# The first gather of a mixture-of-experts layer in two halves, with six more dummy products in the sort before it

## The chip, the core and the metric

The kernel runs on one core of a Trainium2 chip. The metric is the device time of one execution in microseconds (us). One core has a matrix engine (PE, with its weight loads listed apart as PEld), a vector engine (DVE), a scalar engine (ACT), a general engine (POOL) and a queue engine (SP) that issues most of the DMA transfers. Each engine works through its own instructions in program order and waits for others through semaphores.

## The reference

One encoder layer for 512 tokens of width 1024: three token mixers (neighbourhood attention, grouped-query attention, attention into memory tokens) that are gated and summed, a layer norm, a mixture of 16 experts, and a second layer norm. What matters here is the mixture. Each expert chooses its 64 tokens:

```python
def expert_choice_ffn(x, w_router, w_gate_up, w_down):
    B, T, D = x.shape
    cap = EC_CAPACITY_FACTOR * T // N_EXPERTS          # 64
    logits = jnp.einsum('btd,de->bte', x, w_router, ...)
    aff = jax.nn.softmax(logits, axis=-1)
    gate, idx = lax.top_k(jnp.swapaxes(aff, 1, 2), cap)
    xs = x[bidx, idx]                                  # the gather
    h = jnp.einsum('becd,edf->becf', xs, w_gate_up)
    hg, hu = jnp.split(h, 2, axis=-1)
    ye = jnp.einsum('becf,efd->becd', jax.nn.silu(hg) * hu, w_down)
    ye = ye * gate[..., None].astype(ye.dtype)
    return jnp.zeros_like(x).at[bidx, idx].add(ye)
```

Everything is float32. The weights of one expert are 8 MB for gate and up and 4 MB for down.

## The kernel before

The first part of the kernel (to about 500 us) computes the token mixers and the router's logits. Then comes the **sort**: the affinities of all tokens are transposed to one row per expert, and DVE takes the 64 largest of each row, eight at a time (`rounds`, lines 1088 to 1097). The smallest of them is the expert's threshold. It is spread to all partitions by a small product on PE (`thp`, line 1170), DVE compares (`msk`, lines 1174 and 1175), PE counts the chosen tokens with triangular matrices (`cnp`, lines 1179 and 1182), and DVE makes from the counts each chosen token's slot number (`pos`, lines 1184 and 1185).

During the sort PE has little of its own to do. `keep_warm(n)` (line 1110) issues n products of the identity with itself, whose result nobody reads; each is two instructions on PE. One such call, `keep_warm(28)` at line 1156, stands on PE's queue right before `thp`. Two smaller ones stand behind `thp` and behind the counts.

The **gather** is done on PE for a quad of four experts at a time, 256 slots. `onehot(qd)` (line 1194) makes on DVE, for each of the four token blocks, a 128x256 matrix in float16 that is 1 where a token sits in a slot. `gather(qd)` (line 1208) is a generator of nine steps: for each of the eight 128-row pieces f of the model width it multiplies the tokens' high halves (`XH`, line 1216) and low halves (`XL`, line 1218), as stationary operands, with the four one-hot blocks, eight products of 256 columns into a PSUM buffer of the tag "mm" (three buffers), and evicts the sum to `xs` on DVE for even f and on ACT for odd f. The ninth step makes the gate values of the slots: small products into a PSUM tile of the tag "Y" (one buffer, line 1232), which DVE reduces (line 1239) into `gw`.

Then follow the **experts**, e = 0 to 15. `gate_up(e, (k,))` (line 1245) multiplies piece k of `xs` with the weights of gate (g) and up (u), k = 0 to 7. `act_h(e)` applies the activation. `h_transpose(e - 1)` transposes the previous expert's hidden values, and `down(e - 1)` (line 1277) multiplies them with the down weights into a PSUM tile of the tag "Y" (line 1287). In the loop, expert 0 has its eight k steps alone; an expert e from 1 to 14 does k = 0 to 3, with `h_transpose(e - 1)` ahead of k = 3, then `down(e - 1)`, for odd e `slots_T` (line 1307, products of 128 columns from one-hot and identity), and then k = 4 to 7.

The first gather runs three of its steps ahead of expert 0 and the others between expert 0's k steps. The gathers of the other three quads are made at the ends of experts 3, 7 and 11.

The **weights** stream through a ring of twelve SBUF buffers of one or two MB (`RING`, line 32; `class Ring`, line 771; its transfers are issued by SP at line 795). The stream is cut into blocks in the order of use; the first twelve are issued as the buffers come free of what the first part of the kernel held in them. Ten of the twelve buffers are used again. Block 12 and those behind it are issued when PE is done with the block whose buffer they take. Since the order of use is gate and up of expert 0 (k = 0 to 7), gate and up of expert 1 (k = 0 to 3), down of expert 0 (0 to 3), and gate and up of expert 1 (k = 4 to 7), blocks 12 to 15 take the buffers of expert 0's k pairs, 16 and 17 those of expert 1's k = 0, 1 and 2, 3, and 18 that of the last piece of expert 0's down weights and expert 1's k = 4. SP issues in order.

PE's order around the change, before: `keep_warm(28)`, `thp`, `keep_warm(1)`, counts, `keep_warm(4)`, gather steps f = 0, 1, 2, then k = 0, f = 3, k = 1, f = 4, and so on to f = 7 behind k = 4, the gate sums behind k = 5, k = 6, k = 7; then expert 1: k = 0, 1, 2, `h_transpose(0)`, k = 3, `down(0)`, `slots_T(0)`, k = 4 to 7.

Of the kernel before, what the change touches and what calls it, by code (L numbers as in the profile page):

```python
# [11 lines left out]
F16 = mybir.dt.float16  # L12
I32 = mybir.dt.int32
AF = mybir.ActivationFunctionType
ALU = mybir.AluOpType
# [3 lines left out]
P = 128  # L19
# [3 lines left out]
NT = 4  # L23
NEXP = 16
CAP = 64
# [11 lines left out]
A_SCALE = 16384.0  # L37
# [22 lines left out]
def layer_kernel(ctx: ExitStack, tc: tile.TileContext, xt, xn, first0, wu, bgate, rpb, gains, wrt,  # L60
                 lnp, lnt, wx, csn, nmask, tri, iota, out, dbg=None):
    nc = tc.nc
# [12 lines left out]
    def R(tag, shape, name, dt=F32, bufs=None):  # L75
        return rp.tile(shape, dt, name=name, tag=tag, bufs=bufs)
# [3 lines left out]
    def PB(tag, name, shape=(P, 512)):  # L80
        return ps.tile(list(shape), F32, name=name, tag=tag, bufs=PS_BUFS[tag])

    def small(shape, name, dt=F32, bufs=2):
        return sp.tile(shape, dt, name=name, tag=name, bufs=bufs)
# [161 lines left out]
    iota_t = cp.tile([P, CAP], F32, name="iota_t")  # L246
# [636 lines left out]
    pos = rt[:, 1].rearrange("p (m e) -> p m e", m=NT)  # L883
# [162 lines left out]
    def x1_parts(m):  # L1046
        nc.scalar.copy(XH[:, m], x1(m))
        for h in range(2):
            c = slice(h * 512, h * 512 + 512)
            nc.gpsimd.tensor_tensor(XL[:, m, c], x1(m)[:, c], XH[:, m, c], op=ALU.subtract)  # L1050

    xhl = R("G0", [P, 2, NT, D], "xhl", F16)
    XH, XL = xhl[:, 0], xhl[:, 1]
# [45 lines left out]
    def steps(*gens):  # L1099
        for g in gens:  # L1100
            next(g, None)

    def all_of(g):
        for _ in g:
            pass
# [4 lines left out]
    def keep_warm(n):  # L1110
        warm2 = PB("T", "warm2")
        for _ in range(n):
            nc.tensor.matmul(warm2[:, :P], ident, ident, start=True, stop=True)
# [39 lines left out]
    for m in (2, 3):  # L1153
        x1_norm(m)
        x1_parts(m)
    keep_warm(28)
    ring.upto(len(RING))
    dump("aff", aff)

# [31 lines left out]

    OH, XS, GW = {}, {}, {}

    def onehot(qd):
        OH[qd] = oh = R("oh", [P, NT, 256], f"oh{qd}", F16)
        for m in range(NT):
            nc.vector.tensor_tensor(oh[:, m].rearrange("p (e s) -> p e s", e=4),
                                    iota_t[:, None, :].to_broadcast([P, 4, CAP]),
                                    pos[:, m, 4 * qd:4 * qd + 4, None].to_broadcast([P, 4, CAP]), op=ALU.is_equal)

    def split_aff():
        a, b = (R("t", [P, NT * NEXP], n, bufs=2).rearrange("p (m e) -> p m e", m=NT) for n in ("affs", "affr"))
        nc.scalar.activation(aff3[:, :, :, 0], aff, AF.Copy, scale=A_SCALE)
        nc.vector.scalar_tensor_tensor(a, aff, A_SCALE, aff3[:, :, :, 0], op0=ALU.mult, op1=ALU.subtract)
        nc.scalar.copy(aff3[:, :, :, 1], a)
        nc.vector.scalar_tensor_tensor(aff3[:, :, :, 2], a, 1.0, aff3[:, :, :, 1], op0=ALU.mult, op1=ALU.subtract)

    def gather(qd):
        oh = OH[qd]
        xs = [R("hi", [P, 4, 256], f"xs{qd}{j}", bufs=2) for j in range(2)]  # L1210
        XS[qd] = xs
        for f in range(KD):
            g = PB("mm", f"ga{qd}{f}")[:, :256]
            c = slice(f * P, (f + 1) * P)
            for m in range(NT):
                nc.tensor.matmul(g, XH[:, m, c], oh[:, m], start=(m == 0), stop=False)  # L1216
            for m in range(NT):
                nc.tensor.matmul(g, XL[:, m, c], oh[:, m], start=False, stop=(m == NT - 1))
            dst = xs[f // 4][:, f % 4]
            if f % 2:  # L1220
                nc.scalar.activation(dst, g, AF.Identity, bias=lnT[:, 1, f:f + 1], scale=gT[:, f:f + 1])
            else:
                nc.vector.tensor_scalar(dst, g, gT[:, f:f + 1], lnT[:, 1, f:f + 1], op0=ALU.mult, op1=ALU.add)
            yield
        if qd == 0:
            split_aff()
        GW[qd] = gw = small([P, 4], "gw", bufs=2)
        gp2 = PB("Y", f"gw{qd}").rearrange("p (i c) -> p i c", i=2)
        for i in range(0, 4, 2):
            gp = gp2[:, i // 2]  # L1230
            for m in range(NT):
                nc.tensor.matmul(gp[:, 0:6], oh[:, m, i * CAP:(i + 2) * CAP],
                                 aff3[:, m, 4 * qd + i:4 * qd + i + 2].rearrange("p e a -> p (e a)"),
                                 start=(m == 0), stop=(m == NT - 1))
        for i in range(0, 4, 2):
            gp = gp2[:, i // 2]
            for j in range(2):
                for b in (0, 64):
                    nc.vector.tensor_reduce(gw[b:b + 64, i + j:i + j + 1], gp[j * 64:j * 64 + 64, 3 * j:3 * j + 3],
                                            axis=AX.X, op=ALU.add)  # L1240
        nc.vector.tensor_scalar(gw, gw, 0.5 / A_SCALE, None, op0=ALU.mult)

    GU, HT, YP = {}, {}, {}

    def gate_up(e, ks):
        qd, i = divmod(e, 4)
        if ks[0] == 0:
            GU[e] = (PB("S", f"g{e}"), PB("T", f"u{e}"))
        for k in ks:
            w = ring.get("gu", e, k)  # L1250
            xs = XS[qd][k // 4][:, k % 4, i * CAP:(i + 1) * CAP]
            for b in range(2):
                for hf in range(2):
                    nc.tensor.matmul(GU[e][b][hf * 64:hf * 64 + 64], xs,  # L1254
                                     w[b][:, hf * 512:hf * 512 + 512],
                                     start=(k == 0), stop=(k == KD - 1))
            ring.done("gu", e, k)
# [89 lines left out]
    def combine(pr):  # L1347
        yh, yl = YP.pop(pr)
        g = GT.pop(pr)
        for m in range(NT):  # L1350
            for o in range(2):
                c = slice(o * 512, (o + 1) * 512)
                cb = PB("mm", f"cb{pr}{m}{o}")
                nc.tensor.matmul(cb, g[:, m], yh[:, c], start=True, stop=False)
                nc.tensor.matmul(cb, g[:, m], yl[:, c], start=False, stop=True)  # L1355
                a = acc_of(m)[:, c]
                nc.vector.tensor_tensor(a, a, cb, op=ALU.add)  # L1357
                yield

    def rows_of_norm(g2):  # L1360
        for h in range(2):
            bc = ln_row(2, h, f"g2{h}")
            yield
            nc.scalar.copy(g2[:, h * 512:(h + 1) * 512], bc)
# [154 lines left out]
            finish(m, 0)  # L1519
            finish(m, 1)  # L1520

    onehot(0)
    g0 = gather(0)
    steps(g0, g0, g0)
    side = iter(())
    for e in range(NEXP):
        if e == 0:
            for k in range(KD):
                gate_up(0, (k,))
                steps(g0)  # L1530
            all_of(g0)
        elif e < NEXP - 1:
            if e == 2:
                side = residual()
            elif e == 3:
                side = combine(0)
            if e == 12:
                g2 = R("G0", [P, D], "ln2g")
                nc.scalar.copy(ident_r, ident)
                side = rows_of_norm(g2)  # L1540
            for k in range(4):
                if k == 3:
                    h_transpose(e - 1)
                gate_up(e, (k,))
                steps(side, side)
            if e % 2 or e == 12:
                all_of(side)
            down(e - 1)
            if e % 2:
                slots_T(e // 2)  # L1550
            if e % 4 == 3:
                onehot(e // 4 + 1)
            for k in range(4, KD):
                gate_up(e, (k,))
                if e == 2:
                    steps(side, side)
                elif e % 2 == 0 and k > 4:
                    if k == 5:
                        side = combine(e // 2 - 1)
                    steps(side, side, side)  # L1560
            all_of(side)
        else:
            sizes = dict(RING)
            pair, one = sorted(ring.free_at_end[:2], key=lambda t: -sizes[t])
            ap12 = R(pair, [P, 2, 2, NT, 256], "accp12", F32R)
            split_acc(1, ap12[:, 0])
            split_acc(2, ap12[:, 1])
            gate_up(e, range(4))
            x0 = [PB(b, f"xq0{mp}", (P, 2, 256)) for mp, b in enumerate("ST")]
            h_transpose(e - 1)  # L1570
            slots_T(e // 2)
            split_acc(3, R(one, [P, 2, NT, 256], "accp3", F32R))
            gate_up(e, (4, 5))
            x1q = preload(1, ("mm", "mm"))
            gate_up(e, (6, 7))
            spare = PB("mm", "spare")
        act_h(e)
        if e % 4 == 3 and e < NEXP - 1:
            all_of(gather(e // 4 + 1))
# [149 lines left out]
```

## Time and profile before

| | |
|---|---|
| median of 3 runs | 977.68 us (976.96 to 979.64) |
| the profiled execution's own time | 977.92 us |
| its span in the profile | 976.1 us |
| PE busy | 944.4 us (97%) |
| DVE busy | 451.9 us (46%) |
| ACT busy | 274.3 us (28%) |
| POOL busy | 78.4 us (8%) |
| bytes moved by DMA | 251.62 MB, mean 258 GB/s |

Busy times count an engine's instructions; a busy PE is not PE at its peak, since products are pipelined. A row of a timeline or of a group of instructions names the start, the duration, the engine, the line, the operation, the tiles (written <- read), their shapes and how many instructions were merged (x4). A row of windows gives for each stretch the busy time and instruction count of PE, PEld, DVE, ACT and POOL, then the granted clock of PE (1.00 is full speed), the DMA engines' busy share and the GB/s that they moved. Everything is told from one profiled execution.

### The profile page before, as it was taken

The page shows a single profiled execution, that of the slowest core. Times are in us where ns is not written, and L with a number is a line of the kernel's source. Part 1 is how long each engine was busy: PE and PEld are TensorE (multiplying, and loading weights), DVE is VectorE, ACT ScalarE, POOL GpSimd, SP SyncE. Part 2 cuts the span into 40 slices and gives each one's busy share as a digit, 9 for nine tenths or more (in the row PEclk, how much of TensorE's full clock was granted, in tenths as well). Part 3 has the DMA queues.
Part 4 walks back from the last instruction along what each step waited for, and adds up shares of the span by engine and source line. Part 5 has one row for each costly group of instructions (what it writes and reads, how often), then busy time and mean ns, then how long its engine had stood idle before and what let it go on. Part 6 is the DMA issues. An engine that isn't in the chain of part 4 may idle for free.

```text
span 976.1 us, 13068 instructions
## 1 busy us (share of the span) xinstructions
PE 944.4 (97%) x5350; PEld 615.0 (63%) x5350; DVE 451.9 (46%) x857; ACT 274.3 (28%) x540; POOL 78.4 (8%) x86
## 2 busy tenths in 40 slices
PE   8999899999999999999999999999999998997996
PEld 8899787889888888887886333433343332432344
DVE  6347678765376566237464155331332222231426
ACT  5343345444354454323223000100010000100123
POOL 0002403000032231000013000000000000000003
PEclk9999999999999999999999999999999999999998
DMA  9312121111333322584719999999999999999992
GB/s 357 111 68 65 65 65 44 65 44 58 85 117 111 101 82 75 217 325 183 279 50 389 389 422 430 430 433 429 429 430 430 430 430 431 432 429 431 428 419 100
DMA packets 38473, 251.62 MB, mean 258 GB/s; under 512 B 12543, under 2 KB 12927, under 8 KB 24590
## 3 DMA queue, kind: packets, MB, share of 16 engines
q1 hardware_dynamic: 37982, 249.74, 63.5%
q10 hardware_dynamic: 432, 1.05, 0.3%
q8 instruction: 42, 0.69, 0.3%
q14 instruction: 17, 0.14, 0.0%
HBM read 247.89 MB, written 2.10 MB: 256 GB/s over the span
## 4 chain that ended last, share of the span: by engine, by line
PE 70%; DMA 18%; DVE 6%; ACT 2%; POOL 2%; issue 1%; SPq 0%; DVEq 0%; POOLq 0%; ACTq 0%
DMA w<-in_wx 17%; PE g L1254 7%; PE u L1254 7%; PE y L1287 6%; PE gate L269 4%; PE gate L271 4%; PE gate L270 4%; PE nqk L271 1%; PE nqk L270 1%; PE nqk L269 1%; PE gy L627 1%; PE pr L269 1%; PE pr L270 1%; PE pr L271 1%; PE ga L1216 1%
## 5 line engine op out<-in xcount | busy, mean ns | idle before, releaser
L1254 PE MATMUL g<-w,xs 128*64 128x512 f32 x512 | 134.7, 604 | 7.5 <-DMA w<-in_wx 7.5
L1254 PE MATMUL u<-w,xs 128*64 128x512 f32 x512 | 131.6, 592 | 0.0
L1287 PE MATMUL y<-w,hT 128*64 128x512 f32 x480 | 107.0, 594 | 4.6 <-DMA w<-in_wx 3.9
L87 ACT CAST y<-y 64x512 fp32r<-64x512 f32 x30 | 17.4, 579 | 240.3 <-PE y L1287 229.0
L88 DVE TENSOR_TENSOR y<-y,y 64x512 fp32r<-64x512 f32 x30 | 20.7, 689 | 135.2 <-ACT y L87 135.2
L1254 PEld LDWEIGHTS u<-w,xs 128*64 128x64 f32 x512 | 36.8, 137 | 73.1 <-issue 71.7
L1287 PEld LDWEIGHTS y<-w,hT 128*64 128x64 f32 x480 | 33.7, 137 | 74.4 <-issue 63.4
L88 DVE TENSOR_TENSOR los<-raw_twin,whi 128x1024 fp32r<-128x1024 f32 x43 | 54.0, 1257 | 51.3 <-ACT whi L87 51.0
L271 PE MATMUL gate<-xh,los 128*128 128x512 f32 x192 | 74.8, 390 | 0.0
L1254 PEld LDWEIGHTS g<-w,xs 128*64 128x64 f32 x512 | 31.3, 136 | 63.7 <-issue 48.0
L269 PE MATMUL gate<-xh,whi 128*128 128x512 f32 x160 | 63.6, 398 | 0.0
L270 PE MATMUL gate<-xl,whi 128*128 128x512 f32 x160 | 62.4, 390 | 0.0
L1357 DVE TENSOR_TENSOR acc<-acc,cb 128x512 f32<-128x512 f32 x56 | 35.4, 683 | 34.5 <-PE cb L1355 34.5
L87 ACT CAST whi<-raw_twin 128x1024 fp32r<-128x1024 f32 x43 | 45.2, 1051 | 7.3 <-PE wo L1062 4.4
L88 DVE TENSOR_TENSOR los<-raw_twin,los 128x1024 fp32r<-128x1024 f32 x21 | 27.4, 1305 | 36.6 <-ACT los L87 36.5
L1426 POOL TENSOR_TENSOR acc<-acc,ln2g 128x512 f32<-128x512 f32 x6 | 7.6, 1279 | 435.4 <-issue 433.4
L271 PEld LDWEIGHTS gate<-xh,los 128*128 128x128 f32 x192 | 36.1, 188 | 7.7
L603 ACT ACTIVATE att_twin<-gs,nm 128x512 f32<-128x512 f32 x32 | 21.7, 683 | 51.4 <-DVE nm L602 51.4
L1264 ACT ACTIVATE tg<-g 128x512 f32<-128x512 f32 x16 | 9.6, 597 | 94.0 <-PE g L1254 94.0
L1275 DVE COPY hT<-ht 128x512 f32<-128x512 f32 x15 | 10.4, 690 | 54.6 <-PE ht L1272 54.6
L269 PEld LDWEIGHTS gate<-xh,whi 128*128 128x128 f32 x160 | 30.0, 188 | 7.5 <-issue 1.0
L270 PEld LDWEIGHTS gate<-xl,whi 128*128 128x128 f32 x160 | 30.1, 188 | 5.9
(405 smaller groups left out, 1883.9 us busy)
## 6 DMA issues: line engine op xcount, KB each, us to landing
w<-in_wx SPq DMA_DIRECT2D x86, 2048.0 KB
raw_twin<-in_wu SPq DMA_DIRECT2D x65, 512.0 KB
w<-in_wx SPq DMA_DIRECT2D x20, 1024.0 KB
raw<-in_wu SPq DMA_DIRECT2D x8, 512.0 KB
xr<-in_xt SPq DMA_DIRECT2D x4, 512.0 KB
macc<-in_xn SPq DMA_DIRECT2D x2, 1024.0 KB
first<-in_first SPq DMA_DIRECT2D x4, 384.0 KB
bf<-in_rpb SPq DMA_DIRECT2D x64, 24.0 KB
```

The costliest lines, as they stand in the source:

```text
L87: nc.scalar.copy(hi, src)
L88: nc.vector.tensor_tensor(lo, src, hi.bitcast(F32), op=ALU.subtract)
L269: nc.tensor.matmul(acc, w_h, rh[:, k], start=(k == 0), stop=False)
L270: nc.tensor.matmul(acc, w_h, rl[:, k], start=False, stop=False)
L271: nc.tensor.matmul(acc, w_l, rh[:, k], start=False, stop=(k == nk - 1))
L603: nc.scalar.activation(self.p[:, h], self.s[h], AF.Exp, bias=nm[:, h:h + 1], accum_out=self.sm[:, h:h + 1])
L627: nc.tensor.matmul(self.y[h * 64:h * 64 + 64, :P], ST["vg"][:, kc, kvh * 64:kvh * 64 + 64], self.pt[:, h, kc], start=(kc == 0), stop=(kc = ...
L1216: nc.tensor.matmul(g, XH[:, m, c], oh[:, m], start=(m == 0), stop=False)
L1254: nc.tensor.matmul(GU[e][b][hf * 64:hf * 64 + 64], xs, w[b][:, hf * 512:hf * 512 + 512], start=(k == 0), stop=(k == KD - 1))
L1275: nc.vector.tensor_copy(t, tp)
L1287: nc.tensor.matmul(y[o * 64:o * 64 + 64], hT[:, c, hf * 64:hf * 64 + 64], w[j][:, o * 512:(o + 1) * 512], start=(k == 0 and j == 0), stop= ...
L1357: nc.vector.tensor_tensor(a, a, cb, op=ALU.add)
```

## The change

The one-hot and the gather take two more arguments, the first expert of the quad and how many experts, so that a part of the quad's slots can be made. The first quad is made in two halves of 128 slots. The first half (experts 0 and 1) is made where the whole was. The second half's one-hot (experts 2 and 3) is issued on DVE behind the first three steps of the first half; its gather is made in expert 1, two steps behind each of k = 0 to 3, and its gate sums behind the last of these, ahead of `down(0)`. The other three quads are made whole, as before. `keep_warm(28)` becomes `keep_warm(34)`.

```diff
-    keep_warm(28)
+    keep_warm(34)
...
-    def onehot(qd):
-        OH[qd] = oh = R("oh", [P, NT, 256], f"oh{qd}", F16)
+    def onehot(qd, e0=0, n=4):
+        if e0 == 0:
+            OH[qd] = R("oh", [P, NT, 256], f"oh{qd}", F16)
+        oh = OH[qd][:, :, e0 * CAP:(e0 + n) * CAP]
         for m in range(NT):
-            nc.vector.tensor_tensor(oh[:, m].rearrange("p (e s) -> p e s", e=4),
-                                    iota_t[:, None, :].to_broadcast([P, 4, CAP]),
-                                    pos[:, m, 4 * qd:4 * qd + 4, None].to_broadcast([P, 4, CAP]), op=ALU.is_equal)
+            nc.vector.tensor_tensor(oh[:, m].rearrange("p (e s) -> p e s", e=n),
+                                    iota_t[:, None, :].to_broadcast([P, n, CAP]),
+                                    pos[:, m, 4 * qd + e0:4 * qd + e0 + n, None].to_broadcast([P, n, CAP]), op=ALU.is_equal)
...
-    def gather(qd):
+    def gather(qd, e0=0, n=4):
         oh = OH[qd]
-        xs = [R("hi", [P, 4, 256], f"xs{qd}{j}", bufs=2) for j in range(2)]
-        XS[qd] = xs
+        if e0 == 0:
+            XS[qd] = [R("hi", [P, 4, 256], f"xs{qd}{j}", bufs=2) for j in range(2)]
+            GW[qd] = small([P, 4], "gw", bufs=2)
+        xs, gw = XS[qd], GW[qd]
+        sl = slice(e0 * CAP, (e0 + n) * CAP)
         for f in range(KD):
-            g = PB("mm", f"ga{qd}{f}")[:, :256]
+            g = PB("mm", f"ga{qd}{f}")[:, :n * CAP]
             c = slice(f * P, (f + 1) * P)
             for m in range(NT):
-                nc.tensor.matmul(g, XH[:, m, c], oh[:, m], start=(m == 0), stop=False)
+                nc.tensor.matmul(g, XH[:, m, c], oh[:, m, sl], start=(m == 0), stop=False)
             for m in range(NT):
-                nc.tensor.matmul(g, XL[:, m, c], oh[:, m], start=False, stop=(m == NT - 1))
-            dst = xs[f // 4][:, f % 4]
+                nc.tensor.matmul(g, XL[:, m, c], oh[:, m, sl], start=False, stop=(m == NT - 1))
+            dst = xs[f // 4][:, f % 4, sl]
...
-        if qd == 0:
+        if qd == 0 and e0 == 0:
             split_aff()
-        GW[qd] = gw = small([P, 4], "gw", bufs=2)
-        gp2 = PB("Y", f"gw{qd}").rearrange("p (i c) -> p i c", i=2)
-        for i in range(0, 4, 2):
+        gp2 = PB("Y", f"gw{qd}{e0}").rearrange("p (i c) -> p i c", i=2)
+        pairs = range(e0, e0 + n, 2)
+        for i in pairs:
...
-        for i in range(0, 4, 2):
+        for i in pairs:
...
-        nc.vector.tensor_scalar(gw, gw, 0.5 / A_SCALE, None, op0=ALU.mult)
+        gs = gw[:, e0:e0 + n]
+        nc.vector.tensor_scalar(gs, gs, 0.5 / A_SCALE, None, op0=ALU.mult)
...
-    onehot(0)
-    g0 = gather(0)
+    onehot(0, 0, 2)
+    g0 = gather(0, 0, 2)
     steps(g0, g0, g0)
+    onehot(0, 2, 2)
+    g1 = gather(0, 2, 2)
     side = iter(())
...
                 gate_up(e, (k,))
                 steps(side, side)
+                if e == 1:
+                    steps(g1, g1)
+            if e == 1:
+                all_of(g1)
             if e % 2 or e == 12:
                 all_of(side)
             down(e - 1)
```

## The prediction

> **What bounds the kernel now.** I read the page first, then wide windows, the weight queue's issues, and the timeline of the stretch that the diff touches.
>
> ```profile
> span 976.1 us, 13068 instructions
> PEclk9999999999999999999999999999999999999998
> GB/s 357 111 68 65 65 65 44 65 44 58 85 117 111 101 82 75 217 325 183 279 50 389 389 422 430 430 433 429 429 430 430 430 430 431 432 429 431 428 419 100
> PE 70%; DMA 18%; DVE 6%; ACT 2%; POOL 2%; issue 1%; SPq 0%; DVEq 0%; POOLq 0%; ACTq 0%
> ```
>
> PE is busy nearly throughout and leads the chain, so at first sight saved PE time is saved time. The GB/s line says otherwise: from its 24th slice on, the weight stream holds about 430. The chain counts a transfer from issue to landing, so it puts time spent behind other transfers elsewhere; for the second half I trust the windows (after the sum of PE and the other engines: granted clock, DMA share, GB/s).
>
> ```profile
> 512.00:529.00 17.00, 15.79 (x141) 13.25 (x140) 9.56 (x37) 7.34 (x12) 8.33 (x10) 0.90 1.01 429
> 529.00:566.50 37.50, 37.50 (x200) 13.90 (x198) 6.51 (x18) 4.53 (x9) 0.00 (x0) 1.00 0.95 374
> 566.00:946.00 380.00, 367.86 (x1786) 140.42 (x1782) 116.62 (x199) 40.94 (x71) 0.00 (x0) 1.00 1.01 430
> ```
>
> From 566 to 946 us the transfers are saturated. What the change does earlier reaches the end only through one number: **when the stream becomes continuous**. From 529 to 566.5 us it runs at 374, a loss of 37.5 x (1 - 374/430) = 4.9 us. That is the most there is to win. Who holds it back there?
>
> ```profile
> 532.40 0.33 SPq L795 DMA_DIRECT2D w<-in_wx  x1
> 538.09 0.33 SPq L795 DMA_DIRECT2D w<-in_wx  x1
> 543.78 0.33 SPq L795 DMA_DIRECT2D w<-in_wx  x1
> 547.65 0.33 SPq L795 DMA_DIRECT2D w<-in_wx  x1
> 551.09 0.33 SPq L795 DMA_DIRECT2D w<-in_wx  x1
> 555.26 0.33 SPq L795 DMA_DIRECT2D w<-in_wx  x1
> 564.32 0.33 SPq L795 DMA_DIRECT2D w<-in_wx  x1
> SPq L795 <- PE u L1254: 41.3, 9, 9.7
> 532.00:533.00 1.00, 1.00 (x9) 0.65 (x8) 0.00 (x0) 0.00 (x0) 0.00 (x0) 1.00 0.16 66
> 533.00:534.00 1.00, 1.00 (x8) 0.40 (x7) 0.54 (x1) 0.00 (x0) 0.00 (x0) 1.00 0.97 213
> 566.00:567.00 1.00, 1.00 (x6) 0.28 (x4) 0.00 (x0) 0.00 (x0) 0.00 (x0) 1.00 0.80 311
> ```
>
> These seven issues are the ring's blocks 12 to 18. Each waits for PE to finish with the block whose place it takes: 12 to 15 after expert 0's k = 1, 3, 5, 7; 16 and 17 after expert 1's k = 1 and 3; 18 after expert 1's k = 4, which stands behind down(0). Block 12 found the stream dry: 66 and 213 GB/s in the two us after its issue, so an issue must come about 2 us before the last landing. Block 18 came with nothing to spare: the rate dips to 311 just two us after its issue. A PE that reaches that point later delays every later byte; one that reaches it earlier helps only as far as those blocks also land.
>
> **The change part by part.** The sum follows PE from the sort to that point.
>
> ```profile
> 513.25 6.41 PE L1113 MATMUL warm<-ident 128*128 128x128 f32 x56
> 520.59 0.39 PE L1170 MATMUL thp<-dg,rt 16*128 16x16 f32 x2 [0.93 <-ACT dg L1168]
> 522.50:526.00 3.50, 3.50 (x19) 2.81 (x19) 2.08 (x7) 0.00 (x0) 0.00 (x0) 0.51 0.99 414
> 522.74 0.22 DVE L1185 TENSOR_TENSOR rt<-rt 128x64 f32<-128x64 f32 x1
> 522.99 1.43 DVE L1197 TENSOR_TENSOR oh<-iota_t,rt 128x256 f16<-128x256 f32 x4
> L1113 PE MATMUL warm<-ident x94: 271/275/423, 507.9 to 523.6; 128*128 128x128 f32 x94
> L1197 DVE TENSOR_TENSOR oh<-iota_t,rt x16: 409/412/424, 523.0 to 824.0; 128x256 f16<-128x256 f32 x16
> ```
>
> Six dummies are 12 instructions of (6.41 - 0.275)/55 = 0.112 us, 1.34 us. The gap they fill is 0.93 us and ends with thp at 520.59; the last dummy now issues at 519.38 + 1.34 = 520.72, thp can follow at 520.83, so thp, the counts and the one-hot come **0.24 us later**. (Bounds: 0, if the gap swallows them, to 0.41 us, 1.34 less 0.93.)
>
> In return the half clock of 522.5 to 526.0 (0.51) should go. It follows the one stretch of the sort in which PE stands still and then runs tiny products. With the gap filled I take full clock; the other case is a rival below. The Trainium skill, in "TensorE: Matmul & The Clock Gate", Part 1 on the clock gate, has the clock fall only after an idle window of about 3.4 us; by that, 0.93 us could not have cost it and filling the gap could not cure it, and the sum would be 0.8 us higher. The trace disagrees: the clock did fall after 0.93 us.
>
> The one-hot of 128 columns is in no row: between 64 columns (0.22) and 256 (0.41), so 0.28 us; four back to back take 1.43 for 256 (0.41 + 3 x 0.34) and 0.28 + 3 x 0.215 = 0.93 for 128, saving 0.50 (bounds 0.3 to 0.75). The first half is ready at 522.99 + 0.24 + 0.93 = 524.16 instead of 524.42. The second half runs on DVE behind the second eviction, under expert 0's first products, and ends near 527, some 3 us before the next gather that DVE has to evict: nothing.
>
> Now the gathers.
>
> ```profile
> 527.57 1.08 PE L1254 MATMUL g<-w,xs 128*64 128x512 f32 x4
> 529.44 0.61 PE L1216 MATMUL ga<-oh,xhl 128*128 128x256 f16 x4
> 530.42 1.08 PE L1254 MATMUL g<-w,xs 128*64 128x512 f32 x4
> 545.73 1.03 PE L1254 MATMUL g<-w,xs 128*64 128x512 f32 x4
> 547.44 1.03 PE L1254 MATMUL g<-w,xs 128*64 128x512 f32 x4
> L1216 PE MATMUL ga<-oh,xhl x128: 272/273/421, 523.8 to 837.2; 128*128 128x256 f16 x128
> 562.02 0.40 PE L1307 MATMUL gT<-id,oh 128*128 128x128 f16 x4
> L1307 PE MATMUL gT<-id,oh x32: 219/219/231, 562.0 to 929.1; 128*128 128x128 f16 x32
> ```
>
> A k step with a gather takes 530.42 - 527.57 = 2.85, without one 547.44 - 545.73 = 1.71: a gather costs 1.14. Its eight products step (0.61 - 0.273)/3 = 0.11 apart, 0.88; the other 0.26 is the change of operands, paid once per insertion. For 128 columns the same kind of product (f16, own weights) stands in L1307: (0.40 - 0.219)/3 = 0.060, in a short run; half of 0.11 is 0.055. I take 0.057: a half gather costs 0.46 + 0.26, that is **0.42 less** than a whole one. The Trainium skill gives about 81 ns for such pairs at 128 columns ("TensorE: Matmul & The Clock Gate", Back-to-back issue gap); L1307's 60 ns speaks against it, and what it would do is the fourth rival.
>
> Before expert 0's first product stand the rest of the first gather and two more: 21 products from the one-hot's end, 527.57 - 524.42 = 3.15 us at half and whole clock. New: 0.04 + 21 x 0.057 + 0.10 = 1.34. The first product comes at 524.16 + 1.34 = 525.50, **2.07 earlier**. The five gathers inside expert 0 give 5 x 0.42 = 2.1; half the gate sums 0.1. Expert 0 ends **4.27 us earlier**.
>
> Then expert 1 pays. Four pairs of half gathers, one insertion each: 4 x (16 x 0.057 + 0.26) = **4.65**. Evictions lie under the products: a pair fills two of three buffers of "mm" and the next pair is 1.7 us of products away; an eviction takes about half a us. The second gate sums cost 0.1 more, and a new wait.
>
> ```profile
> 543.68 0.35 PE L1232 MATMUL gw<-aff,oh 128*128 128x6 f16 x8
> 544.07 1.36 DVE L1239 TENSOR_REDUCE gw<-gw 64x1 f32<-64x3 f32 x8 [0.50 <-PE gw L1232]
> 530.53 0.56 ACT L1221 ACTIVATE xs<-ga,lnT,gT 128x256 f32<-128x256 f32 x1 [3.16 <-PE ga L1218]
> ```
>
> "Y" has one buffer. In expert 0 its four reductions lay under later products; now down(0), the next user of "Y", stands right behind the sums and waits: drain 0.17, start of DVE 0.04, four reductions of 0.17, 0.05 back, less the 0.13 that PE needs anyway, **0.8 us** (bounds 0.5, if the two engines overlap, to 1.2, if an eviction is still ahead on DVE). Queued behind it on PE are down(0), slots_T and expert 1's k = 4, so block 18.
>
> Issues become: 12 at 529.9, 13 at 534.8, 14 at 539.6, 15 at 543.4, 16 at 548.0, 17 at 554.5, and 18 at 564.32 - 4.27 + 4.65 + 0.1 + 0.8 = **565.6**. At 2.1 MB per block and 430 GB/s (4.88 us) blocks 12 to 17 now run gapless from 532.5 to 561.8, and then the stream stands until about 567.6. The old small gaps are traded for one of 6 us, which ends 1.3 us later than the stream became continuous before. Everything behind is transfer-bound, so the end moves by **+1.3 us**: 977.92 (this profiled execution, span 976.1 and 1.8 around it) + 1.3 = **979.2 us**. The median is 977.68, 0.24 below, and its runs span 976.96 to 979.64.
>
> **The rivals.**
>
> 1. Faster. Block 18 is not what sets the end and the 4.7 us by which block 17 lands earlier (561.8 against 566.5) are kept, less little: 977.9 - 4.5 = 973.4. It needs block 18's issue by 559.8. For: every transfer ahead of it does come earlier. Against: the wait on "PE u" is the queue's own account, and PE's work up to that point does not shrink by 5 us.
>
> 2. The dummies don't hold the clock. From 524.2 to 525.93, 16 products step 0.107 instead of 0.057: +0.8, 980.0. For: counts and tiny products stay as they are. Against: the window before 522.5 gains 1.1 us of work.
>
> 3. The halves are tied together. If a product reading one half of an xs tile waits for evictions into the other, expert 1's k = 1 and 2 each wait for drain 0.22, eviction 0.4 and 0.1 of signals: +1.3, 980.5; more where several such waits meet. Against: the product at 530.42 started before ACT's eviction into the same tile (530.53).
>
> 4. Half gathers don't halve. At 0.081 per product the 21 before expert 0, its 40 and expert 1's 64 cost 125 x 0.024 = 3.0 more: 982.2, slower than the bound below. L1307's row is against it, but only four in a row.
>
> **How the numbers follow.** Forecast 0.50, rivals 0.09, 0.19, 0.15, 0.07. A measurement of this kernel tells about 0.3%, 2.9 us, from no change: 974.8 to 980.6. Slower: all of rival 4, two thirds of 3 (with the bounds of the stall), four tenths of 2, and a fifth of the forecast by its bounds and the runs' own spread: 0.07 + 0.10 + 0.07 + 0.10 = 0.34. Faster: rival 1 and 0.01, 0.10. The rest, 0.56, is within. The forecast's own range is 977.8 to 980.8 (stall -0.3 to +0.4, dummies -0.24 to +0.17, one-hot -0.25 to +0.2, 125 products at 0.055 to 0.060 -0.25 to +0.4, so PE's +1.3 becomes +0.2 to +2.5, and some 0.4 of run to run). For 8 in 10 it must take in rivals 2 and 3 and the edge of 4: 976.6 to 981.9.
>
> **What would show it.** Granted clock 1.0 through 522 to 530; the first expert product near 525.5; k steps of expert 0 at 2.43; the seven issues at the times above, with block 18 near 565.6; a DMA share near 0 around 562 to 567 us; PE waiting on DVE L1239 for 0.8 us before y. If block 18 is issued before 562 us, or the stream is not saturated behind it, the forecast is wrong; if the gathers step 0.08 or products in expert 1 wait for "xs", rivals 4 and 3 decide.

## The result, and the profile after

Over 20 runs of each, side by side, the changed kernel takes 979.76 us (978.14 to 981.44) and the kernel before 977.98 us (976.96 to 980.15). The ratio is 1.0016, with a 95% interval of 1.0009 to 1.0023: 0.9 to 2.2 us slower, inside the 0.3% that the prediction called no change. The profiled execution of the changed kernel took 981.44 us, the slowest of its 20. Its span cannot be set beside that of before, so what follows compares stages.

From the page of the changed kernel (the GB/s are in 40 slices of the span):

```profile
span 979.7 us, 13232 instructions
GB/s 353 93 87 66 65 55 54 65 44 49 89 122 110 102 81 72 219 315 192 278 55 422 412 349 430 431 429 431 428 433 429 430 433 428 430 429 431 429 411 92
PE 71%; DMA 17%; DVE 6%; ACT 2%; POOL 2%; issue 1%; SPq 0%; DVEq 0%; POOLq 0%; ACTq 0%
```

Two slices at 389 have become 422 and 412; the next fell from 422 to 349. PE still leads the chain of waits. The stretches of the changed kernel, in the view of windows, whose columns are those of before:

```profile
12.00:15.50 3.50, 3.50 (x16) 3.50 (x17) 2.53 (x3) 1.05 (x1) 0.00 (x0) 0.51 1.03 423
509.62:589.62 80.00, 77.66 (x530) 38.41 (x528) 32.93 (x92) 15.92 (x30) 9.49 (x10) 1.00 0.95 389
520.68:524.09 3.41, 3.39 (x52) 3.06 (x51) 1.14 (x5) 0.81 (x4) 2.50 (x3) 1.00 0.98 418
524.00:527.40 3.40, 3.40 (x46) 2.75 (x44) 1.99 (x8) 0.46 (x1) 0.00 (x0) 1.00 1.02 431
563.00:564.00 1.00, 1.00 (x6) 0.34 (x4) 0.00 (x0) 0.00 (x0) 0.00 (x0) 1.00 0.81 344
564.00:565.00 1.00, 1.00 (x10) 0.30 (x8) 0.00 (x0) 0.29 (x1) 0.00 (x0) 1.00 0.31 131
566.00:567.00 1.00, 1.00 (x8) 0.29 (x4) 0.35 (x2) 0.94 (x2) 0.00 (x0) 1.00 0.00 0
568.50:948.00 379.50, 366.76 (x1782) 139.91 (x1780) 116.64 (x199) 40.94 (x71) 0.00 (x0) 1.00 1.01 429
```

The first row is half clock at the very start of the program, in a stretch that the change does not touch. It is probably why this execution is late long before the sort: the three profiles with such an early stretch (this one, and halves only and sums early below) issue block 7 at 508.96 to 509.62 us, the eight others at 507.19 to 508.05. The second starts where block 7 of the ring is issued, the eighth transfer: at 509.62 us, against 508.05 before, 1.57 us late for reasons that are not the change's. I therefore count every time from that issue. For comparison, the same view of the kernel before: the early stretch, the 3.41 us ahead of the half clock of its sort, the 80 us from its block 7, and the 60 us behind them:

```profile
12.00:15.50 3.50, 3.50 (x29) 3.50 (x30) 2.92 (x4) 1.71 (x2) 0.00 (x0) 1.00 1.03 421
519.11:522.52 3.41, 2.46 (x43) 2.06 (x43) 1.25 (x6) 0.81 (x4) 2.49 (x3) 1.00 1.00 428
508.05:588.05 80.00, 77.54 (x458) 36.81 (x458) 31.74 (x84) 15.10 (x27) 9.49 (x10) 0.98 0.97 394
588.05:648.05 60.00, 60.00 (x313) 25.48 (x314) 23.74 (x43) 6.35 (x11) 0.00 (x0) 1.00 1.01 430
```

The sort and the start of the experts keep full clock (two rows at 1.00). The six dummies fill the stretch ahead of it: PE is busy for 3.39 of 3.41 us there, before for 2.46. Near 566 us the stream stands still, and from 568.5 us on it is saturated. The weight queue of the changed kernel, blocks 12 to 18, and who released them:

```profile
531.52 0.33 SPq L795 DMA_DIRECT2D w<-in_wx  x1
536.36 0.33 SPq L795 DMA_DIRECT2D w<-in_wx  x1
541.20 0.33 SPq L795 DMA_DIRECT2D w<-in_wx  x1
544.97 0.33 SPq L795 DMA_DIRECT2D w<-in_wx  x1
549.56 0.33 SPq L795 DMA_DIRECT2D w<-in_wx  x1
555.73 0.33 SPq L795 DMA_DIRECT2D w<-in_wx  x1
566.91 0.33 SPq L795 DMA_DIRECT2D w<-in_wx  x1
SPq L795 <- PE u L1260: 35.5, 6, 10.8
```

Less 1.57 these are 529.95, 534.79, 539.63, 543.40, 547.99, 554.16 and 565.34. Predicted were 529.9, 534.8, 539.6, 543.4, 548.0, 554.5 and 565.6. From block 7's issue to block 18's it is 57.29 us; before it was 564.32 - 508.05 = 56.28 (rounding of the times leaves 0.01). I call this distance the **gate**. It grew by 1.01; the prediction had 1.28.

The instructions between, from the timeline of the changed kernel:

```profile
522.51 0.39 PE L1170 MATMUL thp<-dg,rt 16*128 16x16 f32 x2
524.91 0.90 DVE L1199 TENSOR_TENSOR oh<-iota_t,rt 128x128 f16<-128x128 f32 x4
526.59 0.39 PE L1221 MATMUL ga<-oh,xhl 128*128 128x128 f16 x4
527.13 1.08 PE L1260 MATMUL g<-w,xs 128*64 128x512 f32 x4
529.55 1.08 PE L1260 MATMUL g<-w,xs 128*64 128x512 f32 x4
547.58 1.08 PE L1260 MATMUL g<-w,xs 128*64 128x512 f32 x4
550.45 1.08 PE L1260 MATMUL g<-w,xs 128*64 128x512 f32 x4
556.81 0.67 DVE L1244 TENSOR_REDUCE gw<-gw 64x1 f32<-64x3 f32 x4
557.58 7.09 PE L1293 MATMUL y<-w,hT 128*64 128x512 f32 x32 [0.81 <-PE gw L1237]
```

`thp` comes 522.51 - 509.62 = 12.89 us behind block 7, before 520.59 - 508.05 = 12.54: the dummies make it 0.35 late. The one-hot takes 0.90 instead of 1.43. The first expert product comes 527.13 - 509.62 = 17.51 behind block 7, before 527.57 - 508.05 = 19.52: 2.01 earlier. Expert 0's k step with half a gather is 529.55 - 527.13 = 2.42; expert 1's with a pair of halves 550.45 - 547.58 = 2.87. Then `down(0)` waits 0.81 us, while DVE reduces the gate sums. (The row names the products of the sums as what ended the wait; the later of the two are DVE's reductions, which end at 557.48, 0.10 us before `down(0)` starts.)

### The profile page after: what moved, and what is told of

Read it like the earlier page. It is cut to its first block, busy times and chain, and to the rows that moved or that the text cites. A ratio compares the mean times of both kernels' runs of the same rounds, so it can differ in the third digit from the quotient of the medians.

```text
span 979.7 us, 13232 instructions
## 1 busy us (share of the span) xinstructions
PE 947.2 (97%) x5426; PEld 617.6 (63%) x5426; DVE 453.7 (46%) x866; ACT 275.8 (28%) x544; POOL 77.5 (8%) x86
## 4 chain that ended last, share of the span: by engine, by line
PE 71%; DMA 17%; DVE 6%; ACT 2%; POOL 2%; issue 1%; SPq 0%; DVEq 0%; POOLq 0%; ACTq 0%
DMA w<-in_wx 17%; PE g L1260 8%; PE u L1260 7%; PE y L1293 6%; PE gate L269 4%; PE gate L270 4%; PE gate L271 4%; PE nqk L270 1%; PE nqk L269 1%; PE nqk L271 1%; PE gy L627 1%; PE pr L269 1%; PE pr L270 1%; PE pr L271 1%; PE cb L1360 1%
```

## The experiments

Each kernel ran 11 or 12 times beside the kernel before on the same chip. The kernel before took 978.55 us on the chip of the first four, 978.36 on that of the next three, 978.07 on that of the last two. One execution of each was profiled. The table collects the results; its first two rows are the 20 runs of each from above. The rows for the last two columns stand with each kernel: its 80 us window begins at block 7's issue, and the gate is the issue of block 18 less that time. The last column is the GB/s in these 80 us; a rate lower by 1 is 80/430 = 0.19 us of stream less.

| kernel | median, us | ratio to before, 95% interval | gate, us | GB/s |
|---|---|---|---|---|
| before | 977.98 | | 56.28 | 394 |
| changed | 979.76 | 1.0016 (1.0009 to 1.0023) | 57.29 | 389 |
| halves only | 979.70 | 1.0013 (1.0001 to 1.0025) | 56.95 | 392 |
| dummies only | 977.52 | 0.9991 (0.9980 to 1.0002) | 55.90 | 395 |
| sums early | 979.24 | 1.0005 (0.9991 to 1.0018) | 56.44 | 394 |
| late | 977.72 | 0.9986 (0.9975 to 0.9997) | 52.12 | 403 |
| load in expert 1 | 980.13 | 1.0021 (1.0010 to 1.0033) | 58.72 | 382 |
| load in expert 5 | 978.46 | 1.0006 (0.9996 to 1.0016) | 55.57 | 396 |
| spread | 977.68 | 0.9996 (0.9985 to 1.0007) | 52.12 | 414 |
| two quads | 975.40 | 0.9975 (0.9967 to 0.9984) | 52.12 | 413 |
| two quads, 28 dummies | 975.75 | 0.9979 (0.9968 to 0.9990) | 51.77 | 414 |

### The two parts alone

```diff
 halves only: the changed kernel with
-    keep_warm(34)
+    keep_warm(28)
 dummies only: the kernel before with
-    keep_warm(28)
+    keep_warm(34)
```

> The changed kernel with the 28 dummies of before. The marker in all these runs is the time from the ring's eighth issue (block 7, 508.05 us before, 509.62 after) to its nineteenth (block 18, 564.32 and 566.91): 56.28 us before, 57.29 after. Theory (the end moves with block 18's issue): thp comes 0.35 earlier than with 34 dummies, so the marker is 56.9 and the time 0.35 below the changed kernel's 979.8 if the clock stays full; if the clock halves behind the sort, as it did in the profile of before, 0.8 is added: marker 57.7, time 980.2. Rival (the dummies are the whole loss): the time falls to 978.0, that of before.

> The kernel before with 34 dummies in place of 28. Theory: thp 0.35 later; where the clock was half behind the sort it is now full, worth 0.8: marker 55.8, time between 0.5 below the kernel before and, where that one ran at full clock too, 0.35 above it. Rival (the dummies are the whole loss): 1.8 above, 979.8.

Halves only, from the windows the 80 us from block 7, and from the queue block 18:

```profile
508.96:588.96 80.00, 76.73 (x519) 37.11 (x517) 32.91 (x91) 16.23 (x31) 9.49 (x10) 1.00 0.94 392
```

```profile
565.91 0.33 SPq L795 DMA_DIRECT2D w<-in_wx  x1
```

Dummies only, the same two views:

```profile
507.57:587.57 80.00, 78.17 (x470) 37.20 (x470) 32.09 (x84) 15.10 (x27) 9.49 (x10) 1.00 0.97 395
```

```profile
563.47 0.33 SPq L795 DMA_DIRECT2D w<-in_wx  x1
```

The gates came where they were expected, 56.95 and 55.90. The loss lies in the halves: alone they cost 0.1 to 2.4 us by their interval. The dummies alone cost nothing that can be measured (0.998 to 1.0002). What the prediction had not allowed for is the clock: with 28 dummies, halves only ran the sort at 1.00 all the same.

### Is it PE's work, or its place?

Twelve dummies, 24 instructions, ahead of one `down` of the kernel before: ahead of `down(0)`, where they delay block 18, or ahead of `down(4)`, where the stream is saturated. PE's work is the same in both.

```diff
             if e % 2 or e == 12:
                 all_of(side)
+            if e == 1:              # 5 in the other kernel
+                dm = PB("Y", "dm")
+                for _ in range(12):
+                    nc.tensor.matmul(dm[:, :P], ident, ident, start=True, stop=True)
             down(e - 1)
```

> The kernel before with twelve dummy products (24 instructions of 0.112 us, 2.7 us of PE) ahead of down(0) in expert 1. The marker is the time from block 7's issue to block 18's, 56.28 us before. Theory (the end moves with block 18's issue): marker 59.0, time 2.7 above the kernel before, 981.2 against 978.5. Rival (the transfers have slack to take it up): the time of before.

> The same twelve dummies ahead of down(4) in expert 5, where the stream is about 10 us of transfers ahead of its next issue. Theory: PE time there costs nothing: the time of before, 978.5, marker 56.3 or, at full clock behind the sort, 55.5. Rival (PE's work as a whole is the bound, as its share of the chain of waits suggests): 2.7 above, 981.2, as with the dummies in expert 1.

Load in expert 1, first the windows, then the queue:

```profile
507.39:587.39 80.00, 77.17 (x472) 37.67 (x472) 30.70 (x82) 13.95 (x25) 9.50 (x10) 1.00 0.94 382
```

```profile
566.11 0.33 SPq L795 DMA_DIRECT2D w<-in_wx  x1
```

Load in expert 5, the windows, the queue and the first expert product:

```profile
507.75:587.75 80.00, 77.23 (x460) 35.99 (x460) 32.43 (x85) 15.11 (x27) 9.50 (x10) 1.00 0.98 396
522.20:525.70 3.50, 3.19 (x25) 2.35 (x25) 2.41 (x7) 0.00 (x0) 0.00 (x0) 1.00 1.06 438
```

```profile
563.32 0.33 SPq L795 DMA_DIRECT2D w<-in_wx  x1
526.57 1.08 PE L1254 MATMUL g<-w,xs 128*64 128x512 f32 x4
```

The same 24 x 0.112 = 2.7 us of PE work cost 1.0 to 3.2 us in expert 1 (gate 58.72) and could not be told from nothing in expert 5 (-0.4 to +1.6). The two intervals overlap; set directly against each other, the medians of the two kernels lie 1.67 us apart (0.5 to 3.2 by resampling the 12 runs of each). So PE's total work does not set the time here; its work ahead of block 18 does. That also answers why PE's lead in the chain of waits misleads here.

Up to its load the kernel with the load in expert 5 is the kernel before, and it too had full clock (1.00 where before had 0.51): its first expert product comes 526.57 - 507.75 = 18.82 us behind block 7, against 19.52 in the profile of before, and its gate is 55.57 instead of 56.28. Of the five profiles with 28 dummies (the last kernel of the table is the fifth) only that of before has a clock below 1.00 in the 80 us row.

### Which part of the halves

The second half's gate sums go back to expert 0 (sums early). In the kernel called late its gather moves as well, behind expert 1's k = 4 to 7, that is behind the gate, with PE's work the same.

```diff
 sums early:
-    def gather(qd, e0=0, n=4):
+    def gather(qd, e0=0, n=4, sums=4):
...
+        if sums:
+            gate_sums(qd, e0, sums)
+
+    def gate_sums(qd, e0=0, n=4):
...
-    g1 = gather(0, 2, 2)
+    g1 = gather(0, 2, 2, 0)
 late, besides:
                 steps(side, side)
-                if e == 1:
-                    steps(g1, g1)
-            if e == 1:
-                all_of(g1)
...
             for k in range(4, KD):
                 gate_up(e, (k,))
...
+                if e == 1:
+                    steps(g1, g1)
```

> The changed kernel with all gate sums in expert 0 (as before the change), so that nothing of them stands ahead of down(0). Theory: the 0.8 us that PE waits for DVE's reductions goes, and 0.1 of products moves from expert 1 to expert 0: marker 57.29 - 0.85 = 56.4, time about 0.85 below the changed kernel, 978.9. Rival (the wait is covered by something else that is late at the same place, such as the transposed hidden values or an eviction): marker 57.2, time 979.7.

> As the run with the early sums, but the second half's gather stands behind k = 4 to 7 of expert 1, two steps each, and so behind the point that frees block 18's buffer. PE's work is the same. Theory (the end is set by when blocks 18 and next are issued): marker 56.4 - 4.65 = 51.8; block 18 is then no longer late, blocks 19 and 20 are by about 0.8 and 1.0 us, and the time is 2.3 below the kernel before: 975.7. Rival (PE's work as a whole is the bound, wherever it stands): the same time as with the early sums, 978.9.

Sums early, windows and queue:

```profile
509.38:589.38 80.00, 78.47 (x532) 38.21 (x530) 32.98 (x92) 16.50 (x31) 9.48 (x10) 1.00 0.95 394
```

```profile
565.82 0.33 SPq L795 DMA_DIRECT2D w<-in_wx  x1
```

Late, the 80 us, and blocks 18 and 20:

```profile
507.69:587.69 80.00, 77.86 (x530) 37.88 (x529) 32.62 (x90) 15.81 (x30) 9.50 (x10) 1.00 0.98 403
```

```profile
559.81 0.33 SPq L795 DMA_DIRECT2D w<-in_wx  x1
...
571.27 0.33 SPq L795 DMA_DIRECT2D w<-in_wx  x1
```

The wait of `down(0)` is worth 57.29 - 56.44 = 0.85 of the gate, the pairs of half gathers 56.44 - 52.12 = 4.32. (The time of sums early, 979.24, can be told neither from that of before nor from that of the changed kernel.) With the pairs behind the gate, the same work on PE is faster than before by 0.3 to 2.4 us. Its gain, 1.4 us by the ratio, is less than the 2.3 us expected, which the interval still holds: 52.12 against 55.57 is 3.5 us earlier, but only (403 - 396) x 80/430 = 1.3 us more was streamed. The rest is lost behind block 18, where the moved pairs now stand ahead of the release of blocks 19 and 20, as the expectation said. The kernel spread of the next section shows it: its blocks 12 to 18 are issued at the same times behind block 7, within 0.01 us, and its 80 us stream at 414. But its block 19 is issued 55.55 us behind block 7 and its block 20 60.39, in late 57.85 and 63.58. So no block ahead of the gate holds late back.

### Where else the order gates the stream

Spread makes the second half's eight pieces as late as they can be made: behind expert 1's k = 6 and 7, behind expert 2's k = 0 and 1, two ahead of its k = 4, and behind k = 4 and 5. Evictions of a second half are all on ACT.

```diff
 spread, against sums early:
-            if f % 2:
+            if f % 2 or e0:
...
-                if e == 1:
-                    steps(g1, g1)
-            if e == 1:
-                all_of(g1)
+                if e == 2 and k < 2:
+                    steps(g1)
...
+            if e == 2:
+                steps(g1, g1)
             for k in range(4, KD):
...
+                if e == 1 and k > 5 or e == 2 and k < 6:
+                    steps(g1)
```

> The early sums, and the second half's gather one step at a time: f = 0 and 1 behind k = 6 and 7 of expert 1, 2 and 3 behind k = 0 and 1 of expert 2, 4 and 5 behind down(1), 6 and 7 behind k = 4 and 5; its evictions all on ACT, since DVE works on the residual there. Theory: each block from 12 to 26 is then issued at least 2 us before the stream runs dry, but where the issue comes only 2 to 3.5 us ahead a block took 5.0 to 5.4 us instead of 4.9 in the runs so far, so of the 4.9 us lost before, 1.5 to 2 stay: the time is about 3 below the kernel before, 975.5. Rival (moving the work gains no more than in the run with the late gather, because expert 2's products then wait for the evictions): 977.5.

Spread, windows of the 80 us, the 60 us behind them and a part of those, then blocks 18, 20 and 33 of the queue:

```profile
507.19:587.19 80.00, 77.54 (x515) 37.05 (x514) 31.72 (x88) 17.20 (x33) 9.51 (x10) 1.00 0.99 414
587.19:647.19 60.00, 60.00 (x324) 25.79 (x323) 21.63 (x40) 7.28 (x13) 0.00 (x0) 1.00 0.99 417
626.00:646.00 20.00, 20.00 (x112) 8.01 (x110) 4.17 (x14) 2.29 (x4) 0.00 (x0) 1.00 0.97 400
```

```profile
559.31 0.33 SPq L795 DMA_DIRECT2D w<-in_wx  x1
...
567.58 0.33 SPq L795 DMA_DIRECT2D w<-in_wx  x1
...
630.24 0.33 SPq L795 DMA_DIRECT2D w<-in_wx  x1
```

This was a miss: 975.5 was expected, 977.68 measured. In the first 80 us it streams 414, the (414 - 396) x 80/430 = 3.3 us that were hoped for. It loses (430 - 417) x 60/430 = 1.8 of them right behind: the stream, now ahead, runs into a second gate, block 33, issued at 630.24. PE reaches its release behind the whole gather of the second quad, 8 x 0.88 = 7.0 us of products in one piece at the end of expert 3. In the kernel before, whose stream stood later, the same place cost nothing: 430 in the 60 us behind its 80. The rival of the expectation, a wait of expert 2 for an eviction, happens once, for 1.49 us at 585.27; it is not the cause, since the stream moves 433 GB/s from 586 to 606 us, and two quads has the same wait.

The next kernel makes that gather in halves too: experts 4 and 5 where the whole was, experts 6 and 7 one step behind each k of expert 5.

```diff
 two quads, against spread:
+                if e == 5:
+                    steps(gq)       # in both loops over k
...
-            all_of(gather(e // 4 + 1))
+            if e == 3:
+                all_of(gather(1, 0, 2))
+                gq = gather(1, 2, 2, 0)
+            else:
+                all_of(gather(e // 4 + 1))
 two quads, 28 dummies, besides:
-    keep_warm(34)
+    keep_warm(28)
```

> The spread kernel, with the second quad's gather in halves as well: the half for experts 4 and 5 at the end of expert 3, where the whole was, the other one step behind each k of expert 5. In the spread kernel the stream moved 414 GB/s in the 80 us behind block 7's issue (394 before), but 417 in the next 60 (430 before): it ran dry again at block 33, whose issue waits for PE behind that second gather. Theory (that is a second gate of the same kind, and half a gather is 8 x 0.42 = 3.4 us of PE earlier): 414 and 430, and the time 3.5 below the kernel before, about 974.9. Rival (the first 80 us gained only by borrowing from the next, so the stream is bound by something else, such as its own rate): 417 or less in the 60 us again, time about 977.5.

> The same with 28 dummies in the sort. Theory: thp comes 0.34 earlier, at full clock expert 0 starts 0.34 earlier, and 0.5 later in an execution whose clock halves behind the sort (one of the four profiles with 28 dummies so far); the stream's first 80 us change by 1 or 2 GB/s, the time by less than 0.4. Rival (the dummies matter more than by their place, through the clock): over 0.8 above the run with 34.

Two quads, windows, and blocks 18 and 33:

```profile
507.76:587.76 80.00, 77.54 (x515) 37.05 (x514) 31.72 (x88) 17.20 (x33) 9.50 (x10) 1.00 0.99 413
587.76:647.76 60.00, 59.90 (x336) 24.42 (x335) 22.80 (x42) 6.84 (x13) 0.00 (x0) 1.00 1.01 426
```

```profile
559.88 0.33 SPq L795 DMA_DIRECT2D w<-in_wx  x1
...
627.65 0.33 SPq L795 DMA_DIRECT2D w<-in_wx  x1
```

Two quads with 28 dummies, the 80 us and block 18:

```profile
507.90:587.90 80.00, 76.61 (x509) 36.04 (x508) 31.72 (x87) 17.21 (x33) 9.50 (x10) 1.00 0.99 414
```

```profile
559.67 0.33 SPq L795 DMA_DIRECT2D w<-in_wx  x1
```

In two quads block 33 comes at 627.65 - 507.76 = 119.89 us behind block 7, in spread at 630.24 - 507.19 = 123.05, and the 60 us stream at 426 instead of 417. At 975.40 us, 1.6 to 3.2 us below the kernel before, this kernel **beats both**. It does not reach the 430 and the 3.5 us expected; what holds the rest back is open. The six dummies make no difference to its median that can be measured: 975.75 without them, and the intervals overlap. They may matter to the clock of single runs (see the clock, below).

## Why the prediction was right

**The bound.** It held. In the kernel before and in the changed one the stream is saturated behind block 18, and PE's work counts only ahead of it: shown by the two loads and by late against sums early. (Once block 18 comes earlier, later issues become gates, as late and spread show.) The first rival (block 18 not the gate, 973.4) has fallen.

**The gate, step by step.** First product 2.07 earlier predicted, 2.01 measured; k step of expert 0 2.43 and 2.42; wait for the gate sums 0.8 and 0.81; all seven issues within 0.4 us. A pair of half gathers adds 2.87 - 1.71 = 1.16; the prediction's 16 x 0.057 + 0.26 is 1.17. Two terms were off. The dummies cost 57.29 - 56.95 = 0.34, not 0.24 (its upper bound was 0.41). The four pairs cost 4.32 by sums early against late, not 4.65 (the terms of that sum give 4.69). The starts of expert 1's k steps and of `down(0)` in these two traces show where: the pairs add 1.11, 1.14, 0.91 and 1.10 us. The cheap one stands beside `h_transpose`, which changes the operands anyway. That one change of operands is saved there is argued, not shown.

**The clock.** Here a credit was too large. The prediction gave the six dummies the end of the half clock, worth about 0.7 to 0.8 us, as if every run had it. But four of five profiles with 28 dummies had full clock behind the sort without them, though PE is busy for the same 2.45 or 2.46 us of the 3.41 us ahead in all five; in such a run there is nothing to gain. That the dummies do nothing for the clock does not follow. The mean granted clock of a whole run is on record for every run of the experiments: 0.995 or 0.996 in the profiled runs with one stretch of half clock ahead of their last 10 us, 0.997 or 0.998 in those with none. It is 0.994 or less in 30 of the 135 runs with 28 dummies and in one of the 79 with 34. In two quads with 28 dummies five of 12 runs have it, with a median of 977.63 us against 975.20 of the other seven; with 34 none of 11 has. So the dummies seem to spare some runs a low clock, which a median hides; in which stretch these runs lose it is not recorded.

Against the gate of a profile with full clock and otherwise the code of before, 55.57, the change costs 57.29 - 55.57 = 1.72, made of 56.95 - 55.57 = 1.38 for the halves and 0.34 for the dummies. Of the stream that is (396 - 389) x 80/430 = 1.3 us, against 0.9 from the profile of before; the medians lie 1.78 apart, with an interval of 0.9 to 2.2 that holds both. The forecast's +1.28 of the gate was so 0.44 too low: the credit of about 0.7 and the 0.1 of the dummies, less what the pairs were priced too high. That these errors partly cancel is luck, and it is chance that the one profile of before was one with the half clock. The time, 979.76 against 979.2, is 0.56 above the forecast. The Trainium skill ("TensorE: Matmul & The Clock Gate", Part 1) asks for an idle window of about 3.4 us, free-running; the half clock of before lasted about that long (0.51 over 3.5 us) but followed 0.93 us of standing still and tiny products, so the length agrees and the condition does not. (In the same part the Trainium skill also tells of a kernel whose frequent short pauses made the clock swing, without a length for them.) The free-running window would explain why the same gap costs the clock in one run and not in four; no run here tests it.

**The stream ahead of the gate.** Dry from 561.8 us, said the prediction. The rows of 563 to 565 (344, then 131) put it at about 564.3, less 1.57 at 562.7: six blocks in 562.7 - 532.5 = 30.2 us are 5.0 us each, if they began when predicted, instead of 4.88. That costs nothing here, because block 18 comes later anyhow.

**The other rivals.** The clock held (second). No product of expert 1 waited for an eviction into its tile (third). The half gathers step (0.39 - 0.22)/3 = 0.057 apart, the price taken, so 0.081 per product (fourth, and the Trainium skill's figure for pairs at 128 columns) does not hold here. The row with the shortest product of both sizes, in the changed kernel's view of one line:

```profile
L1221 PE MATMUL ga<-oh,xhl x160: 216/272/283, 525.3 to 839.9; 128*128 128x256 f16 x96, 128*128 128x128 f16 x64
```

**What stays open.** Behind block 18 the profiles differ by some 3 us without an order that I can name: span less issue is 411.8 in before, 412.8 in the changed kernel, 411.6 with the load in expert 1, 414.5 with the load in expert 5, whose profiled run (979.58) lay 1.1 above its own median. In that last one the queue shows a part of it: one issue, at 880.33 us, waits 6.0 us for an earlier landing, where the longest such wait of before from 870 to 885 us is 4.5; why is open. A single profile's span is therefore no measure of effects of this size; the gates and the medians are.

## What to carry to other kernels

Where a weight stream is saturated to the end, look for the last transfer that had to wait for a free buffer: work ahead of its release costs time (2.7 us of products cost 1.0 to 3.2 here), and the same work behind it is free as long as no later issue waits for it. Deferring work past one product only to put it in front of the next gate trades small gaps for a larger one; it has to go past the gate, and then the next gate has to be looked for. A price taken from a single profiled run, such as a dip of the clock, should be seen in a second profile before it is credited, and looked for in the spread of the runs as well as in their median.

## What the runs showed of the hardware

The granted clock is not a property of the code alone: the same 28 dummies and the same gap gave 0.51 over 3.5 us in one profile and 1.00 in four, and the changed kernel shows 0.51 from 12.0 to 15.5 us, where the kernel before has 1.00 with the same code.

Four profiles show one stretch of half clock each ahead of their last 10 us (before from 522.52, the changed kernel from 12.04, halves only from 99.57, sums early from 99.48). Each lasts 3.41 us. In the 3.41 us ahead of each, PE is busy for 2.46, 1.96, 1.60 and 1.60 us, and its longest standstill is 0.93, 0.87, 1.81 and 1.81 us. Other profiles pass the same stretches, as little busy, at full clock, so a half idle stretch is not enough by itself.

Float16 products of 128 columns, each with its own weights, keep a step of 0.057 us, half that of 256 columns (0.11), so halving a gather costs only the change of operands (0.2 to 0.26 us for each insertion).
